# Hybrid retention and attention step on Trainium2: the last two feed-forward columns and the output phase in a written order

## The chip, the cores and the metric

The kernel is one program on one core of a Trainium2 chip. The metric is the device time of one execution in microseconds. The kernel before took 1125.89 us (median of 3 runs, 1125.66 to 1126.71). A core has TensorE for matmuls (PE in the profile, with PEld for its weight loads), VectorE (DVE), ScalarE (ACT) and GpSimd (POOL) for elementwise work, and SyncE (SP), which here only issues DMAs. Each engine works through a queue of its own in order, and waits on semaphores for the others.

## The reference, cut to what matters

640 tokens of width 1024 (128 of a prompt and 512 latent ones) go through one layer of a diffusion backbone. The change touches only its end: the gated feed-forward part with a convolution of width 3 over the tokens, its gated residual, and the last norm.

```python
def conv_ffn(h, w_up, conv_w, conv_b, w_down):
    L = h.shape[1]
    u = h @ w_up
    up = jnp.pad(u, ((0, 0), (1, 1), (0, 0)))
    uc = conv_w[0] * up[:, :L] + conv_w[1] * up[:, 1:L + 1] + conv_w[2] * up[:, 2:L + 2] + conv_b
    a, g = jnp.split(uc, 2, axis=-1)
    return (jax.nn.silu(g) * a) @ w_down
...
        xs = xs + g2 * conv_ffn(h, w_up[l], conv_w[l], conv_b[l], w_down[l])
...
    y_prompt = rmsnorm(xp, final_g)
    y_sample = rmsnorm(xs, final_g)
```

Here `rmsnorm(x, g)` is x times the reciprocal root of its mean square, times the weight g. The hidden width is 2816, so `w_up` has 2 x 2816 columns and `w_down` 2816 rows.

## The kernel before, in words

Matrices are multiplied in float32 as three products of split numbers (`mm3`, lines 158 to 161): each factor is a rounded high part and a low part that holds the rest. ScalarE makes the high part (a cast), and the low part is a difference, made by VectorE (L152), or by ScalarE and an adding DMA on GpSimd's queue (L149, L150; the argument `"dma"`).

The hidden width is cut into 22 columns of 128, numbered f = 0 to 21. For a column, the two halves of the up-projection (i = 0 the value, i = 1 the gate) are computed for pairs of columns by seven products of quarter matrices (`unit_group`, a Strassen-like scheme; products 1, 5, 6, 2, 3, 7, 4). Products 7 and 4 finish the two columns of a pair: product 7 the odd one, product 4 the even one. Then `conv(f, i)` does the convolution (one ScalarE step L1583, two VectorE steps L1584 and L1585), and `gate(f)` the gated product (tanh on ScalarE L1595, two VectorE steps L1596 and L1597, the high part on ScalarE L1598, the low part on VectorE L1599). The results feed the down-projection: five blocks of tokens t = 0 to 4 times two halves of the output width (c0 = 0 and 512). A bank of PSUM holds one such half (128 x 512).

`seq` is the written order of TensorE's work (`manual_schedule(engines={ET.PE})`). An engine that is named there keeps the order of the code; engines that are not named are ordered by the framework's planner, by readiness in its own estimate of times. While an item of `seq` runs, `pump` issues loads and splits of weights ahead, and `later` holds convolutions and gates that are popped one at a time. A unit's last product (product 4) is held back by two items of the next group.

The last four columns, 18 to 21, are multiplied at the end. `last_group(g)` accumulates the columns 18 and 19 (parts 0 and 1 of `fs`) for t = 0, 2, 1, 3 and both halves in eight banks while the gates of 20 and 21 are still being made. In the old order product 4 of the last unit comes after t=0 and t=2 of the first of these groups.

The output phase then has VectorE and TensorE in a written order. For each half, `last_mm` adds the columns 20 and 21 to the bank (`(4, ...)` has no bank yet and takes all four parts), `down_add` multiplies the bank by the residual gate `gb` into a temporary (L1671) and adds it to x1 (L1676), and `square` has ScalarE sum the squares (L1693, two rows of the profile). When all halves of a block are there, `root_sum` adds the partial sums (L1701), has GpSimd raise them to -0.5 (L1702) and VectorE scale them (L1703), and `root` refines that by one Newton step (L1710 to L1714). `out` stores a half: with `fused`, VectorE multiplies by the root and by the norm's weight `fg` in one step (L1725); otherwise ScalarE multiplies by the root alone (L1727), and the weight must have been multiplied in before, by `gain` on GpSimd (L1720). In the old order `gain` is done for three halves, (0, 0), (1, 0) and (2, 0), and seven halves are fused.

Of the kernel before, what the change touches and what calls it, by code (L numbers as in the profile page):

```python
# [9 lines left out]
F32 = mybir.dt.float32  # L10
# [8 lines left out]
P = 128  # L19
# [53 lines left out]
def hybrid_step(ctx: ExitStack, tc: tile.TileContext, a: dict, o: dict):  # L73
# [1506 lines left out]
    def conv(f, i):  # L1580
        u, q = ub[f % 2][i], i * NF + f
        v = cvs[f, i] = x_row()[:, :641]
        nc.scalar.activation(v, u[:, 1:642], AF.Identity, scale=cw[:, 1, q:q + 1], bias=cw[:, 3, q:q + 1])  # L1583
        V.scalar_tensor_tensor(v, u[:, 0:641], cw[:, 0, q:q + 1], v, op0=ALU.mult, op1=ALU.add)  # L1584
        V.scalar_tensor_tensor(v, u[:, 2:643], cw[:, 2, q:q + 1], v, op0=ALU.mult, op1=ALU.add)  # L1585

    gts = {}

    def gate(f):
        if f // 2 not in gts:  # L1590
            gts[f // 2] = gt_pair()
        r = [x[:, f % 2, 15:656] for x in gts[f // 2]]
        ca, cg = cvs[f, 0], cvs[f, 1]
        tg = t7([P, 641], tag="tg", bufs=1)
        nc.scalar.activation(tg, cg, AF.Tanh, scale=0.5)  # L1595
        V.scalar_tensor_tensor(cg, tg, 1.0, cg, op0=ALU.add, op1=ALU.mult)  # L1596
        V.tensor_mul(ca, ca, cg)  # L1597
        nc.scalar.copy(r[0], ca)  # L1598
        V.tensor_sub(r[1], ca, r[0].bitcast(F32))  # L1599

# [153 lines left out]
    def unit_group(p, i):  # L1754
# [34 lines left out]
        def prod(m):  # L1789
            def go():  # L1790
# [24 lines left out]
                elif m == 4:  # L1815
                    nc.scalar.copy(his[0], ps)
# [55 lines left out]
    def last_group(g):  # L1872
# [11 lines left out]

        def prep(h):
            def go():
                w = w_split(st["raw"][h], 2, 512, "dma" if h else None)
                ws[g] = [x + y for x, y in zip(ws.get(g, ([], [])), w)]
            return go

        items = [lambda t=t: last_mm(t, g * 512, 512, (0, 1)) for t in (0, 2, 1, 3)]
        return load, [(prep(0), 2, items)], items, prep(1)
# [3 lines left out]
    seq, held = [], []  # L1896
    for _, _, items in groups:
        for x in items[:-1] if len(items) == 7 else items:
# [4 lines left out]
        if len(items) == 7:  # L1903
            held.append((2, items[-1]))
# [21 lines left out]
    with tc.manual_schedule(engines={ET.PE}):  # L1926
        pump(0)
        for n, item in enumerate(seq):
# [7 lines left out]
    for fn in later:  # L1936
        fn()
    for e in ends:
        e[3]()

    fg = wp([P, 4 * 512], F32, tag="raw", bufs=2)[:, :DM]
    nc.sync.dma_start(fg, a["final_g"].unsqueeze(0).to_broadcast([P, DM]))
    with tc.manual_schedule(engines={ET.DVE, ET.PE}):
        def last(t, c0, n):
            last_mm(t, c0, n, (2, 3) if t < NT - 1 else (0, 1, 2, 3))
            down_add(bank[t, c0], t, c0)
            square(t, c0, n)
# [24 lines left out]
        out(3, 512, True)  # L1972
        out(3, 0, True)
# [37 lines left out]
```

## Time and profile before

| | us |
|---|---|
| median of 3 runs | 1125.89 |
| the profiled execution, its time | 1125.21 |
| the profiled execution, its span | 1123.3 |
| TensorE busy | 1098.1 |
| VectorE busy | 871.4 |
| ScalarE busy | 636.5 |
| GpSimd busy | 165.4 |

The span runs from the first to the last instruction of the profiled execution. In a row of the timeline, the first column is the start in microseconds from the span's start, the second the duration, then engine, line of the kernel, operation, output and inputs by the program's names, shape, and in brackets the idle time of the engine before it and what ended it. Engines overlap the end of one instruction with the start of the next, so starts can lie before the end of the row above.

### The profile page before, as it was taken

What the parts mean: (1) busy time and instruction counts of PE and PEld (TensorE: products, weight loads), DVE (VectorE), ACT (ScalarE), POOL (GpSimd) and SP (SyncE); (2) the same over time, 40 slices, a digit from 0 to 9 for tenths busy, and PEclk for the clock granted to TensorE, in tenths of its full rate; (3) what the DMA queues carried; (4) which work ended last, traced back from release to release, by engine and by line L of the source; (5) the groups of instructions that cost most, each with busy time, mean ns of one, the idle gap of its engine ahead of it and who ended that gap; (6) DMA issues with size and microseconds to landing.
All of it is one profiled execution on the core that took longest, in us unless ns stands there. A gap on an engine that the chain in (4) does not pass through costs nothing.

```text
span 1123.3 us, 17862 instructions
## 1 busy us (share of the span) xinstructions
PE 1098.1 (98%) x6757; PEld 1003.3 (89%) x6757; DVE 871.4 (78%) x1513; ACT 636.5 (57%) x1269; POOL 165.4 (15%) x190
## 2 busy tenths in 40 slices
PE   5999999999999999999999999999999999999996
PEld 4788899999989878899999889999899999899995
DVE  4677877668969969768887559968688597589888
ACT  5356656554234235768766336678466476575463
POOL 0042200000000011022113122012111111121012
PEclk9999999999999999999999999999999999999999
DMA  9742111016855726746669837457657656676552
GB/s 306 254 142 84 42 39 38 1 38 215 287 190 155 245 72 141 98 75 123 129 134 187 293 133 178 114 117 145 147 131 175 132 97 148 132 132 167 124 131 94
DMA packets 147109, 156.85 MB, mean 140 GB/s; under 512 B 28216, under 2 KB 117384, under 8 KB 146768
## 3 DMA queue, kind: packets, MB, share of 16 engines
q1 hardware_dynamic: 110880, 119.65, 33.8%
q0 software_dynamic: 35872, 35.95, 20.7%
q8 instruction: 53, 0.87, 0.3%
q14 instruction: 32, 0.26, 0.1%
q10 hardware_dynamic: 272, 0.11, 0.0%
HBM read 115.71 MB, written 8.67 MB: 111 GB/s over the span
## 4 chain that ended last, share of the span: by engine, by line
PE 90%; DVE 4%; ACT 2%; DMA 2%; issue 1%; SPq 1%; ACTq 0%; DVEq 0%
DMA p0.u4.4_116<-in_w_mod 1%; DVE x1.u1.1_6541 L1676 1%; DMA weights.raw.266_7937<-in_w_down 0%; DMA xin.u1.1_72<-in_c_ctx 0%; SPq L331 0%; DVE x1.u1.1_6541 L1725 0%; PE mm3.mm.57_5730 L1149 0%; DVE x1.u1.1_6541 L1483 0%; PE mm3.mm.72_6381 L1149 0%; DVE acts.u2.2_91 L432 0%; PE mm1.mm.11_294 L161 0%; PE mm7.mm.8_7748 L1799 0%; PE mm3.mm.69_6246 L1152 0%; PE mm3.mm.66_6117 L1152 0%; PE mm7.mm.50_10241 L1798 0%
## 5 line engine op out<-in xcount | busy, mean ns | idle before, releaser
L816 POOL DMA_DIRECT2D spill.u2.2_2891<-f1.s.1_1160 x1 | 0.6, 592 | 129.8 <-DVE mod.u3.3_2846 L604 129.8
L1813 DVE TENSOR_TENSOR t7.u4.4_7029<-t7.u4.4_7029,const.u1.1_70 128x320 f32<-128x320 f32 x10 | 4.9, 493 | 11.0 <-ACT const.u1.1_70 L1812 11.0
L429 ACT CAST acts.u1.1_90<-f0.s.2_104 128x640 fp32r<-128x640 f32 x4 | 2.9, 728 | 9.5 <-DVE f0.s.2_104 L427 9.5
L152 DVE TENSOR_TENSOR weights.wh.113_4462<-weights.raw.111_4459,weights.wh.112_4461 128x1024 fp32r<-128x1024 f32 x1 | 1.2, 1226 | 8.6 <-ACT weights.wh.112_4461 L147 8.6
L299 POOL DMA_DIRECT2D mod.acc.25_3630<-in_b_mod x2 | 1.7, 848 | 42.2 <-ACT ret.u4.4_3422 L874 42.2
L584 POOL TENSOR_TENSOR p1.u1.1_604<-p1.u3.3_608,p1q.u1.1_598 128x512 f32<-128x512 f32 x1 | 1.3, 1311 | 44.1 <-DMA p1.vc.6_613<-in_cache_v 44.1
L1001 DVE SCALAR_TENSOR_TENSOR ret2.u1.1_4272<-ret2.u1.1_4272,const.u10.10_86 64x128 f32<-64x128 f32 x24 | 6.6, 381 | 1.2 <-ACT ret2.u1.1_4272 L994 1.1
L147 ACT CAST weights.wh.67_3284<-weights.raw.66_3282 128x1024 fp32r<-128x1024 f32 x1 | 1.0, 1048 | 11.3 <-PE mm3.mm.8_3125 L198 11.3
L147 ACT CAST weights.wh.77_3520<-weights.raw.76_3518 128x1024 fp32r<-128x1024 f32 x1 | 1.1, 1051 | 11.2 <-PE mm3.mm.16_3382 L198 11.2
L553 ACT ACTIVATE f0.s.3_710<-f0.s.3_710,p1q.ny20.11_878 128x128 f32<-128x128 f32 x20 | 6.0, 389 | 2.5 <-DVE p1q.ny20.11_878 L220 2.5
L553 ACT ACTIVATE p1.u4.4_610<-p1.u4.4_610,p1.ny10.15_660 128x128 f32<-128x128 f32 x10 | 3.0, 388 | 7.6 <-DVE p1.ny10.15_660 L220 7.6
L429 ACT CAST acts.u1.1_90<-f0.s.1_103 128x640 fp32r<-128x640 f32 x4 | 2.9, 726 | 7.8 <-DVE f0.s.1_103 L427 7.7
L446 PE MATMUL aux1.aux.1_134<-const.u1.1_70,xin.u1.1_72 80*128 80x80 f32 x1 | 0.4, 367 | 7.0 <-DMA xin.u1.1_72<-in_b_mod 7.0
L999 DVE SCALAR_TENSOR_TENSOR ret2.u1.1_4272<-ret2.u1.1_4272,const.u10.10_86 64x128 f32<-64x128 f32 x24 | 6.7, 336 | 0.5 <-ACT ret2.u1.1_4272 L992 0.5
L1235 ACT ACTIVATE rt.u1.1_5123<-rt.u1.1_5123 128x640 f32<-128x640 f32 x8 | 5.9, 740 | 1.5 <-DVE rt.u1.1_5123 L1163 1.5
L1720 POOL TENSOR_TENSOR x1.u1.1_6541<-x1.u1.1_6541,weights.raw.441_11100 128x512 f32<-128x512 f32 x3 | 4.9, 1636 | 12.2 <-ACT x1.tm.111_11113 L1693 9.4
L1687 DVE TENSOR_TENSOR x1.u1.1_6541<-x1.u1.1_6541,gate.u1.1_6527 128x512 f32<-128x512 f32 x10 | 6.7, 685 | 0.0
L269 ACT ACTIVATE mod.wm.41_4253<-aux3.aux.5_4243 128x512 f32<-128x512 f32 x1 | 0.6, 597 | 10.6 <-issue 10.6
L446 PEld LDWEIGHTS aux1.aux.1_134<-const.u1.1_70,xin.u1.1_72 80*128 80x128 f32 x1 | 0.2, 182 | 7.0 <-issue 7.0
L152 DVE TENSOR_TENSOR weights.wh.83_3656<-weights.raw.81_3653,weights.wh.82_3655 128x1024 fp32r<-128x1024 f32 x1 | 1.2, 1226 | 6.6 <-ACT weights.wh.82_3655 L147 6.6
L299 POOL DMA_DIRECT2D mod.acc.34_3970<-in_b_mod x2 | 1.5, 759 | 31.7 <-PE mm3.mm.31_3941 L161 31.5
L553 ACT ACTIVATE f0.s.4_959<-f0.s.4_959,p1q.ny20.20_1127 128x128 f32<-128x128 f32 x20 | 6.2, 399 | 0.0
(6860 smaller groups left out, 5029.7 us busy)
## 6 DMA issues: line engine op xcount, KB each, us to landing
spill.u1.1_2890<-x1.u1.1_6541 POOLq DMA_DIRECT2D x5, 512.0 KB, 3.8
xin.u2.2_102<-in_x_sample SPq DMA_DIRECT2D x4, 512.0 KB, 4.6
p0.u5.5_119<-in_w_mod SPq DMA_DIRECT2D x2, 1024.0 KB, 9.7
p0.u6.6_125<-in_w_mod SPq DMA_DIRECT2D x2, 1024.0 KB, 14.2
p0.u7.7_128<-in_w_mod SPq DMA_DIRECT2D x2, 1024.0 KB, 12.3
gate.u1.1_6527<-spill.u3.3_2892 SPq DMA_DIRECT2D x2, 1024.0 KB, 10.9
x1.u1.1_6541<-in_x_sample SPq DMA_DIRECT2D x4, 512.0 KB, 6.9
out_y_sample<-x1.u1.1_6541 SPq DMA_DIRECT2D x8, 256.0 KB, 2.2
```

The lines of the kernel that those rows point to most:

```text
L147: nc.scalar.copy(hi, rv)
L152: (lo_eng or V).tensor_sub(lo, rv, hi.bitcast(F32))
L299: nc.gpsimd.dma_start(accs[v][0:1, c, :], a["b_mod"][0:1, col:col + DM], accum_op=ALU.add)
L429: nc.scalar.copy(hT[0][:, k, :], xk)
L553: nc.scalar.activation(x[:, j], x[:, j], AF.Copy, scale=rstd[:, j:j + 1])
L999: V.scalar_tensor_tensor(Ss[0:64, hh, st + 1, j], Ss[0:64, hh, st, j], cdsel[0:64, h:h + 1], Ss[0:64, hh, st + 1, j], op0=ALU.mult, op1=AL ...
L1001: V.scalar_tensor_tensor(Ss[64:128, hh, 2 - st, j], Ss[64:128, hh, 3 - st, j], cdsel[64:128, h:h + 1], Ss[64:128, hh, 2 - st, j], op0=ALU. ...
L1235: nc.scalar.activation(x, x, AF.Tanh, scale=0.5)
L1676: V.tensor_add(x1[:, t, gs], x1[:, t, gs], down_mul(ps, t, c0))
L1687: V.tensor_mul(x1[:, t, gs], x1[:, t, gs], gb[:, t == 0, gs])
L1720: eng.tensor_mul(x, x, fg[:, c0:c0 + 512])
L1813: V.tensor_sub(his[1], his[1], u3[i])
```

## The change

It has three parts. First, `conv` and `gate` are cut into generators, so that their steps can be interleaved; for the last two columns the tanh goes into the tile `ub` of the column's own up-projection, in place of the one tile `tg`. Second, the last two columns are written out in a fixed order for TensorE, VectorE and ScalarE: product 7, the item t=0 of the first group, product 4, then the steps of the two columns in turn; the second half of the last weights is split by ScalarE and VectorE in that order (`prep_parts`) instead of by ScalarE and the adding DMA. The half (3, 512) isn't begun ahead any more, so its columns 18 and 19 are multiplied in the output phase. Third, the output phase has another order, now for ScalarE too, and `gain` is done for six halves: (0, 0), (1, 0), (2, 0), (2, 512), (3, 0) and (4, 0); four halves are fused.

```diff
-    def conv(f, i):
+    def conv_parts(f, i):
         u, q = ub[f % 2][i], i * NF + f
         v = cvs[f, i] = x_row()[:, :641]
         nc.scalar.activation(v, u[:, 1:642], AF.Identity, scale=cw[:, 1, q:q + 1], bias=cw[:, 3, q:q + 1])
+        yield
...
+    def conv(f, i):
+        run(conv_parts(f, i))
...
-    def gate(f):
+    def gate_parts(f):
...
-        tg = t7([P, 641], tag="tg", bufs=1)
+        tg = t7([P, 641], tag="tg", bufs=1) if f + 2 < NF else ub[f % 2][1][:, 1:642]
         nc.scalar.activation(tg, cg, AF.Tanh, scale=0.5)
+        yield
         V.scalar_tensor_tensor(cg, tg, 1.0, cg, op0=ALU.add, op1=ALU.mult)
         V.tensor_mul(ca, ca, cg)
+        yield
         nc.scalar.copy(r[0], ca)
+        yield
         V.tensor_sub(r[1], ca, r[0].bitcast(F32))
...
-                    if i and (p % 2 == 0 or p == 1):
+                    if i and (p % 2 == 0 or p == 1) and f0_ + 2 < NF:
                         later.extend([lambda: gate(f0_ + 1), lambda: gate(f0_)])
...
+        def prep_parts():
+            rv = st["raw"][1][:, :1024]
+            hi, lo = (wp([P, 1024], F32R, tag="wh", bufs=8) for _ in range(2))
+            nc.scalar.copy(hi, rv)
+            yield
+            V.tensor_sub(lo, rv, hi.bitcast(F32))
+            put([[x[:, :512], x[:, 512:]] for x in (hi, lo)])
+
+        items = [lambda t=t: last_mm(t, g * 512, 512, (0, 1)) for t in ((0, 2, 1, 3), (0, 2, 1))[g]]
+        return load, [(prep(0), 2, items)], items, prep_parts() if g else prep(1)
...
-        for n, item in enumerate(seq):
+        cut = pos[id(last_unit[-2])]
+        for n, item in enumerate(seq[:cut]):
...
+        for fn in later:
+            fn()
+        later.clear()
+        pump(cut + 2)
+        assert not preps and loaded == len(groups)
+        ends[0][3]()
...
+    with tc.manual_schedule(engines={ET.PE, ET.DVE, ET.Activation}):
+        seq[cut]()
+        f1_, f0_ = NF - 1, NF - 2
+        c1_ = conv_parts(f1_, 1)
+        next(c1_)
+        seq[cut + 2]()
+        seq[cut + 1]()
+        c0_ = conv_parts(f0_, 1)
+        next(c0_)
+        next(ends[1][3])
+        run(c1_)
+        g1_ = gate_parts(f1_)
+        next(g1_)
+        run(c0_)
+        g0_ = gate_parts(f0_)
+        next(g1_)
+        next(g0_)
+        next(g1_)
+        next(g0_)
+        run(g1_)
+        next(g0_)
+        run(g0_)
+        run(ends[1][3])
+        for item in seq[cut + 3:]:
+            item()
...
         for t in range(3):
-            last(t, 0, 512)
+            down_part(t, 0, 512)
             gain(t, 0, nc.gpsimd)
-            last(t, 512, 512)
-        last(3, 0, 512)
+        for t in range(3):
+            down_part(t, 512, 512)
+        gain(2, 512, nc.gpsimd)
+        down_part(3, 0, 512)
+        gain(3, 0, nc.gpsimd)
         root_sum(0, 3)
-        last(3, 512, 512)
         root(0, 3)
         out(0, 0)
-        last(4, 0, 512)
         out(1, 0)
+        down_part(3, 512, 512)
+        out(2, 0)
+        out(2, 512)
+        out(0, 512, True)
+        out(1, 512, True)
         root_sum(3, 1)
-        out(0, 512, True)
-        last(4, 512, 256)
-        last(4, 768, 256)
-        out(2, 0)
+        down_part(4, 0, 512)
+        gain(4, 0, nc.gpsimd)
         root(3, 1)
-        out(1, 512, True)
+        out(3, 0)
+        down_part(4, 512, 256)
+        out(3, 512, True)
+        down_part(4, 768, 256)
         root_sum(4, 1)
-        out(2, 512, True)
         root(4, 1)
+        out(4, 0)
         out(4, 512, True)
-        out(4, 0, True)
-        out(3, 512, True)
-        out(3, 0, True)
```

`down_part` is the old `last` (the matmuls of a half, `down_add`, `square`); it takes all four parts where the half has no bank yet.

More of the change, by code (lines that the diff above doesn't have):

```diff
@@ L1896, in hybrid_step @@
     seq, held = [], []
+    last_unit = groups[-3][2]
     for _, _, items in groups:
-        for x in items[:-1] if len(items) == 7 else items:
+        for x in items[:-1] if len(items) == 7 and items is not last_unit else items:
             seq.append(x)
@@ L1902, in hybrid_step @@
                 seq.append(held.pop(0)[1])
-        if len(items) == 7:
+        if len(items) == 7 and items is not last_unit:
             held.append((2, items[-1]))
@@ L1935, in hybrid_step @@
                 later.pop(0)()
[L1936 to L1947, printed above, removed]
+        for fn in later:
+            fn()
```

17 lines of the change are left out of this document (11 added, 6 removed).

## The prediction

> **What bounds the kernel now.** I read the page first (engine totals, then the chain that ended last), then the windows of the output phase, then the timelines of the engines around it. The page says that TensorE is the bound of nearly the whole span:
>
> ```profile
> PE 1098.1 (98%) x6757; PEld 1003.3 (89%) x6757; DVE 871.4 (78%) x1513; ACT 636.5 (57%) x1269; POOL 165.4 (15%) x190
> PE 90%; DVE 4%; ACT 2%; DMA 2%; issue 1%; SPq 1%; ACTq 0%; DVEq 0%
> ```
>
> The change touches only the last 40 us, so what counts is which engine ends last there. The windows view (busy time and, in brackets, instructions) splits the output phase; of its rows, the part up to the first `root` and the tail after the last `down_add`:
>
> ```profile
> 1098.75:1110.87 12.12, 12.12 (x54) 9.78 (x53) 11.77 (x19) 5.07 (x14) 5.80 (x4) 1.00 0.01 1
> ...
> 1115.28:1123.30 8.02, 0.00 (x0) 0.00 (x0) 4.86 (x12) 0.51 (x2) 0.55 (x1) 0.66 0.61 231
> ```
>
> VectorE is busy for 11.77 of the first 12.12 us, while GpSimd has 5.80 and ScalarE 5.07: this phase belongs to VectorE, and the tail to VectorE, then to the last stores. Its start is set by TensorE, whose timeline has no gap before it:
>
> ```profile
> 1088.66 0.31 PE L1799 MATMUL mm7.mm.59_10879<-acts.u1.1_90,weights.wh.434_10917 128*128 128x320 f32 x1
> ...
> 1095.78 0.39 PE L159 MATMUL mm7.mm.65_11082<-weights.wh.435_10951,gt.gt0.25_10753 128*128 128x512 f32 x1
> ...
> 1097.17 0.39 PE L159 MATMUL acc7.acc.51_11002<-weights.wh.437_11090,gt.gt0.27_11040 128*128 128x512 f32 x1
> ...
> 1098.55 0.39 PE L159 MATMUL acc7.acc.53_11061<-weights.wh.439_11095,gt.gt0.27_11040 128*128 128x512 f32 x1
> ```
>
> Six matmuls make half a bank, 1.39 us (1095.78 to 1097.17 to 1098.55). VectorE's timeline then shows how the handover goes and what one half costs it:
>
> ```profile
> 1097.10 0.83 DVE L1599 TENSOR_TENSOR gt.gt1.28_11041<-x1.row.107_10933,gt.gt0.27_11040 128x641 fp32r<-128x641 f32 x1 [0.79 <-ACT gt.gt0.27_11040 L1598]
> 1098.75 0.69 DVE L1671 TENSOR_TENSOR x1.tm.110_11110<-acc7.acc.51_11002,gate.u1.1_6527 128x512 f32<-128x512 f32 x1 [0.82 <-PE acc7.acc.51_11002 L161]
> 1099.48 0.69 DVE L1676 TENSOR_TENSOR x1.u1.1_6541<-x1.u1.1_6541,x1.tm.110_11110 128x512 f32<-128x512 f32 x1
> 1100.14 0.69 DVE L1671 TENSOR_TENSOR x1.tm.112_11122<-acc7.acc.53_11061,gate.u1.1_6527 128x512 f32<-128x512 f32 x1
> ```
>
> The last gate result is there at 1097.93, so VectorE waits for TensorE (0.82 us), and from 1098.75 it needs 1.39 us a half (1098.75 to 1100.14) for the L1671 multiply and the L1676 add. Third, GpSimd's products by `fg` are not free for VectorE:
>
> ```profile
> 641.69 1.29 POOL L1483 TENSOR_TENSOR x1.u1.1_6541<-x1.u1.1_6541,x1.tm.4_6631 128x512 f32<-128x512 f32 x1 [8.47 <-DVE x1.tm.4_6631 L1482]
> ...
> 1101.06 1.65 POOL L1720 TENSOR_TENSOR x1.u1.1_6541<-x1.u1.1_6541,weights.raw.441_11100 128x512 f32<-128x512 f32 x1 [9.39 <-ACT x1.tm.111_11113 L1693]
> 1107.19 1.60 POOL L1720 TENSOR_TENSOR x1.u1.1_6541<-x1.u1.1_6541,weights.raw.441_11100 128x512 f32<-128x512 f32 x1 [1.44 <-ACT x1.tm.119_11159 L1693]
> ```
>
> ```profile
> 1108.27 1.08 DVE L1676 TENSOR_TENSOR x1.u1.1_6541<-x1.u1.1_6541,x1.tm.122_11179 128x512 f32<-128x512 f32 x1
> 1109.27 0.15 DVE L1701 TENSOR_REDUCE t7.rm.28_11184<-x1.u3.3_6543 128x3 f32<-128x12 f32 x1
> ...
> 1110.87 0.16 DVE L1712 TENSOR_TENSOR t7.rt.31_11201<-t7.ry.30_11186 128x3 f32<-128x3 f32 x1
> ```
>
> A 512-wide product takes GpSimd 1.29 us where VectorE leaves it alone, 1.65 and 1.60 here: it first waits for the running L1676. The next L1676 (1108.27) takes 1.08 instead of 0.69 and ends 0.56 after GpSimd's end (1107.19 + 1.60 = 1108.79). The two engines exclude each other when both read two tiles of SBUF; L1671, which reads PSUM, runs on beside GpSimd. So seven halves with three products take 1109.35 - 1098.75 = 10.60 us.
>
> **The change, part by part. 1: TensorE.** The item t=3 of the second group goes, and its six matmuls come back in front of `(3, 512)`. The output phase starts one half earlier: 1098.75 - 1.39 = **1097.36**. The moved matmuls cost nothing: TensorE would end `(3, 512)` at 1097.16 + 8 halves of 1.39 = 1108.3, and VectorE, as worked out below, wants it at 1111.8.
>
> **2: the two columns.** The start holds only if the gates keep up. Rows of the old order:
>
> ```profile
> 1084.77 1.05 ACT L147 CAST weights.wh.439_11095<-weights.raw.433_10900 128x1024 fp32r<-128x1024 f32 x1
> 1085.72 0.93 ACT L1583 ACTIVATE x1.row.108_10998<-t7.u4.4_7029,const.u13.13_89 128x641 f32<-128x641 f32 x1
> 1089.17 0.41 ACT L1816 COPY t7.u2.2_7027<-mm7.mm.59_10879 128x320 f32<-128x320 f32 x1
> ...
> 1090.44 0.91 ACT L1583 ACTIVATE x1.row.109_11029<-t7.u2.2_7027,const.u13.13_89 128x641 f32<-128x641 f32 x1
> 1093.84 0.74 ACT L1595 ACTIVATE t7.tg.27_11055<-x1.row.109_11029 128x641 f32<-128x641 f32 x1 [1.87 <-DVE x1.row.109_11029 L1585]
> ```
>
> ```profile
> 1079.90 1.22 DVE L152 TENSOR_TENSOR weights.wh.436_10952<-t7.rawl.25_10898,weights.wh.435_10951 128x1024 fp32r<-128x1024 f32 x1
> ...
> 1087.60 0.89 DVE L1585 SCALAR_TENSOR_TENSOR x1.row.108_10998<-t7.u4.4_7029,const.u13.13_89,x1.row.108_10998 128x641 f32<-128x641 f32 x1
> ```
>
> Before, a cast stood ahead of either convolution: that of 1084.77 before 1085.72, and a second between 1089.17 and 1090.44. Now product 4 ends one half sooner, 1088.97 - 1.39 = 1087.6; its copy 0.41, the convolution 0.93 and one cast 1.05 bring ScalarE to 1090.0, the first tanh to 1090.7. VectorE does the two L1585-like steps of column 20 by 1090.8 (0.89 each), the gate of column 21 by 1092.5 (0.83 a step, as L1599), that of column 20 by 1094.1, the two low parts by 1094.9 and 1095.7. TensorE wants column 21 at 1095.8 and column 20's low part, in its third matmul, at 1097.0. Product 4 also takes the bank of product 7 again; that one's copy (0.41) is hidden by the 1.39 of the item t=0 between them. The weights' low part, now on VectorE instead of GpSimd's DMA, costs 1.22 (L152) and ends at 1096.9, before the first output multiply. All hidden, with 0.5 to 1.2 us to spare; beyond that, each microsecond late is a microsecond of start. The tanh tile put into `u` waits for nothing new: the convolution has read it by then. The `fg` load waits for the same buffer as before and stays hidden by the six halves.
>
> **3: up to the first root.** Seven halves with three products again: the last L1676 ends at 1097.36 + 10.60 = 1107.96, the sixth one about 1.39 sooner, 1106.57. A product starts 0.89 after its add's end (1099.48 + 0.69 to 1101.06, the square between), so the product of `(2, 512)` runs from 1107.46 for 1.65 to 1109.11. Behind it on GpSimd's queue stand the product of `(3, 0)` and the power of `root_sum(0, 3)`:
>
> ```profile
> 1109.50 0.89 POOL L1702 TENSOR_TENSOR t7.ry.30_11186<-t7.rm.28_11184,const.u1.1_70 128x3 f32<-128x3 f32 x1 [0.71 <-DVE t7.rm.28_11184 L1701]
> ```
>
> That power took 0.89 on an idle GpSimd. The planner, not the diff, orders the two. If the product is first, the power ends at 1109.11 + 1.29 + 0.89 = 1111.3. If the power is first, it ends at 1110.0 and the product follows at once, while `root`'s first instruction (L1712) reads two tiles. Who then gets the port is shown by an older place, where a GpSimd instruction releases VectorE and has another behind it:
>
> ```profile
> 97.53 1.90 POOL L562 TENSOR_TENSOR p1q.sw.14_911<-f0.s.3_710,p1q.u3.3_600 128x256 f32<-128x256 f32 x2
> ```
>
> ```profile
> 97.61 1.22 DVE L564 TENSOR_TENSOR f0.s.3_710<-f0.s.3_710,p1q.u2.2_599 128x512 f32<-128x512 f32 x1 [2.05 <-POOL p1q.sw.13_902 L562]
> 98.86 1.12 DVE L565 TENSOR_TENSOR f0.s.3_710<-f0.s.3_710,p1q.sw.13_902 128x512 f32<-128x512 f32 x1
> ```
>
> The VectorE step starts at 97.61, after GpSimd's next one, and takes 1.22 where one of 512 takes 0.68 to 0.69: it is held. So root starts at 1111.3 either way. Before, L1671 and L1676 of `(3, 512)` stood between `root_sum` and `root` and covered the power; now nothing does, and the written order holds VectorE from 1108.2 to 1111.3, **3.1 us**, with every `down_part`, and behind it ScalarE's first `out`, queued up. With 0.49 for root (1110.87 to 1111.36 below) `(3, 512)` starts at 1111.8.
>
> **4: the rest.**
>
> ```profile
> 1111.36 0.69 DVE L1671 TENSOR_TENSOR x1.tm.126_11220<-acc7.acc.55_11207,gate.u1.1_6527 128x512 f32<-128x512 f32 x1
> ...
> 1113.61 0.42 DVE L1671 TENSOR_TENSOR x1.tm.128_11248<-acc7.acc.56_11235,gate.u1.1_6527 128x256 f32<-128x256 f32 x1
> ...
> 1114.40 0.42 DVE L1671 TENSOR_TENSOR x1.tm.130_11266<-acc7.acc.57_11253,gate.u1.1_6527 128x256 f32<-128x256 f32 x1
> 1114.85 0.43 DVE L1676 TENSOR_TENSOR x1.u1.1_6541<-x1.u1.1_6541,x1.tm.130_11266 128x256 f32<-128x256 f32 x1
> 1115.20 0.21 DVE L1710 SCALAR_TENSOR_TENSOR t7.rt.35_11273<-t7.ry.34_11229,t7.rh.33_11228 128x1 f32<-128x1 f32 x1
> 1115.52 0.75 DVE L1725 SCALAR_TENSOR_TENSOR x1.u1.1_6541<-x1.u1.1_6541,t7.ry.30_11186,weights.raw.441_11100 128x512 f32<-128x512 f32 x1
> 1116.18 0.15 DVE L1701 TENSOR_REDUCE t7.rm.36_11278<-x1.u3.3_6543 128x1 f32<-128x4 f32 x1
> 1116.44 0.74 DVE L1725 SCALAR_TENSOR_TENSOR x1.u1.1_6541<-x1.u1.1_6541,t7.ry.30_11186,weights.raw.441_11100 128x512 f32<-128x512 f32 x1
> ...
> 1117.54 1.41 DVE L1725 SCALAR_TENSOR_TENSOR x1.u1.1_6541<-x1.u1.1_6541,t7.ry.38_11280,weights.raw.441_11100 128x512 f32<-128x512 f32 x2
> 1118.88 1.41 DVE L1725 SCALAR_TENSOR_TENSOR x1.u1.1_6541<-x1.u1.1_6541,t7.ry.34_11229,weights.raw.441_11100 128x512 f32<-128x512 f32 x2
> ```
>
> `(3, 512)` 1.39; two fused outputs at 0.66 (1115.52 to 1116.18); `root_sum` 0.26 (1116.18 to 1116.44); `(4, 0)` 1.39; root 0.32 (1115.20 to 1115.52); `(4, 512)` 0.79 (1113.61 to 1114.40): 1111.8 + 5.47 = 1117.3, its add still running to 1117.35. GpSimd's product of `(4, 0)` has waited since about 1117.1. In the row at 98.86 the waiting GpSimd instruction came between two VectorE steps (1.12 instead of 0.68), so I take it to come first: to 1118.65, then the rest of the fused output 0.56 and `(4, 768)` 0.88 (two steps of 0.43 and a gap) less an overlap of 0.07. The last add ends at 1120.0; were VectorE never held, at 1118.8. From there the tail has one fused output left. ScalarE's last row of the old tail is the end of the square:
>
> ```profile
> 1115.70 0.19 ACT L1693 ACTIVATION_READ_ACCUMULATOR x1.tm.131_11269<-x1.u1.1_6541 128x1 f32 x1
> ```
>
> So: 0.61 from the last add's end to the square's (1115.28 to 1115.89), 0.08 to the reduce, 1.36 from reduce to fused output (1116.18 to 1117.54), 0.75 for it, and 3.01 from VectorE's last end to the span's end (1118.88 + 1.41 = 1120.29 to 1123.30): 5.81. Here the change gains: the old tail took 8.02 (1115.28 to 1123.30), since three more fused outputs stood in it.
>
> **Sum:** 1120.0 + 5.8 = 1125.8, against 1123.3: -1.4 by the start, -2.2 by the tail, +3.1 by the wait, the rest by fused outputs moved ahead and by held steps. That is 2.5 us more. The profiled execution took 1125.21 (1.91 outside its span), the median is 1125.89: **1128.3 us, slower by 0.2%**.
>
> The Trainium skill, GPSIMD Engine Reference, section 3.1, gives about 2.6 cycles an element for a two-input step of GpSimd, at 1.2 GHz an estimate of 1.11 us for 512; three products stand in my chain, so the sum would be 0.5 us lower by it. The trace has 1.29, and I stay with that.
>
> **The rivals.** (a) VectorE keeps the port and GpSimd's last product fits beside L1671: end of adds 1118.8, **1127.1 us**. For it: VectorE's steps start 0.07 before the old one ends. Against: the row at 98.86. (b) Not slower: the power comes first on GpSimd and L1712 gets the port before the product behind it. Root starts at 1110.1, 1.2 sooner, less 0.4 for an add held as at 1108.27: **1127.5**, with (a) **1126.3**, no change. It decides at one point, whether VectorE's first instruction after the power starts before GpSimd's next; the row at 97.61 speaks against it. The Trainium skill, SBUF — State Buffer, section "Who interferes with whom", says that the first to start holds the shared port for its whole instruction; the held rows agree, and leave open who is first. (c) Faster: GpSimd holds nobody up, because the power is placed ahead of the product of `(2, 512)` and nothing is held: seven halves take 7 x 1.39 = 9.7, root starts at 1108.2, the adds end 7.5 later at 1115.7, and the last two stores, which no longer follow two others within 2.75 us, may land 0.5 sooner (an estimate): **1123.6**. Against it: the product is ready 0.6 us before the power. (d) The columns are late by more than they have to spare, because the written order makes one engine wait for another at each step: +1.5 us, **1129.8**.
>
> **Chances.** Forecast 0.43 (from 1127.6 to 1129.0; by 0.30 above the line), (a) 0.17, (b) 0.13, (c) 0.14 (0.11 of it faster), (d) 0.13. A measurement of this kernel tells about 0.2%, 2.25 us, from no change. Slower: 0.30 + 0.13 = 0.43; faster 0.11; the same 0.46, since the forecast stands close to the line. The range from 1124.9 to 1129.9 leaves out most of (c) and half of (d).
>
> **What would show it.** Right: the first L1671 near 1097.4; a gap of VectorE near 3 us between `root_sum(0, 3)` and L1712, released by GpSimd; a fused output of over 1 us beside GpSimd's sixth product; 5.8 us from the last add to the end. Wrong: L1712 within 1 us of the reduce, products of GpSimd with no longer VectorE step beside them, or a gap of TensorE before the output phase.

## The result, and the profile after

| | us |
|---|---|
| before, median of 12 runs | 1125.89 (1125.46 to 1126.97) |
| changed, median of 12 runs | 1128.66 (1127.81 to 1128.88) |
| ratio | 1.0022, 95% interval 1.0013 to 1.0031 |
| changed, the profiled execution, its time and its span | 1128.41 and 1126.5 |

The changed kernel is 2.77 us (0.2%) slower. Line numbers have moved: the multiply by the gate is L1681 (L1671 before), its add L1686, the square L1703, the steps of `root_sum` L1711 (reduce), L1712 (power, GpSimd) and L1713 (scale), those of `root` L1720 and L1722 to L1724, the product by `fg` on GpSimd L1730, the fused output L1735, ScalarE's output L1737, the store L1739.

From the page of the changed kernel, the engine totals and the chain that ended last:

```profile
PE 1099.1 (98%) x6757; PEld 1004.1 (89%) x6757; DVE 873.1 (78%) x1511; ACT 639.0 (57%) x1271; POOL 170.0 (15%) x192
PE 89%; DVE 4%; ACT 3%; issue 1%; DMA 1%; POOL 0%; ACTq 0%; SPq 0%; POOLq 0%; DVEq 0%
```

GpSimd has 4.6 us more than before (three more products), VectorE 1.7 more, although three fused outputs went: the low part of the last weights has come to it (1.22, the row of 1096.31 below), and a held instruction counts as busy. The windows of the output phase, cut at the first step of `root` and at the end of the last add, as before:

```profile
1098.07:1110.70 12.63, 12.63 (x56) 10.19 (x55) 11.46 (x16) 5.08 (x14) 7.55 (x6) 1.00 0.01 1
1110.70:1120.17 9.47, 4.06 (x30) 3.63 (x28) 9.19 (x18) 5.01 (x11) 3.12 (x3) 0.95 0.51 194
1120.17:1126.50 6.33, 0.00 (x0) 0.00 (x0) 1.44 (x5) 1.23 (x3) 0.55 (x1) 0.50 0.33 124
```

The first window hardly grew (12.63 against 12.12 us), but it holds seven halves and a wait where it held eight halves; the tail fell from 8.02 to 6.33, and the middle doubled, from 4.41 to 9.47. From the first multiply to the span's end it is 28.43 us where it was 24.55, 3.88 more, of which the earlier start gives back 1.4.

VectorE's timeline shows where the time is (L1906 is the low part of the last weights, the last step of the two columns):

```profile
1096.31 1.22 DVE L1906 TENSOR_TENSOR weights.wh.440_11031<-weights.raw.432_10881,weights.wh.439_11030 128x1024 fp32r<-128x1024 f32 x1
...
1098.07 0.69 DVE L1681 TENSOR_TENSOR x1.tm.110_11100<-acc7.acc.51_11008,gate.u1.1_6527 128x512 f32<-128x512 f32 x1 [0.54 <-PE acc7.acc.51_11008 L161]
...
1107.98 0.69 DVE L1686 TENSOR_TENSOR x1.u1.1_6541<-x1.u1.1_6541,x1.tm.122_11170 128x512 f32<-128x512 f32 x1
1108.59 0.16 DVE L1711 TENSOR_REDUCE t7.rm.26_11176<-x1.u3.3_6543 128x3 f32<-128x12 f32 x1
1108.78 1.08 DVE L1713 TENSOR_SCALAR t7.rh.27_11177<-t7.rm.26_11176 128x3 f32<-128x3 f32 x1
1110.70 1.25 DVE L1722 TENSOR_TENSOR t7.rt.29_11182<-t7.ry.28_11178 128x3 f32<-128x3 f32 x1 [0.84 <-POOL t7.ry.28_11178 L1712]
1111.98 0.16 DVE L1723 TENSOR_TENSOR t7.rt.29_11182<-t7.rt.29_11182,t7.rh.27_11177 128x3 f32<-128x3 f32 x1
...
1112.26 0.68 DVE L1681 TENSOR_TENSOR x1.tm.124_11203<-mm7.mm.65_11190,gate.u1.1_6527 128x512 f32<-128x512 f32 x1
...
1113.59 1.41 DVE L1735 SCALAR_TENSOR_TENSOR x1.u1.1_6541<-x1.u1.1_6541,t7.ry.28_11178,weights.raw.441_11092 128x512 f32<-128x512 f32 x2
...
1117.61 1.76 DVE L1735 SCALAR_TENSOR_TENSOR x1.u1.1_6541<-x1.u1.1_6541,t7.ry.32_11218,weights.raw.441_11092 128x512 f32<-128x512 f32 x1
...
1119.74 0.43 DVE L1686 TENSOR_TENSOR x1.u1.1_6541<-x1.u1.1_6541,x1.tm.130_11279 128x256 f32<-128x256 f32 x1
...
1122.07 0.75 DVE L1735 SCALAR_TENSOR_TENSOR x1.u1.1_6541<-x1.u1.1_6541,t7.ry.36_11286,weights.raw.441_11092 128x512 f32<-128x512 f32 x1
```

and GpSimd's, beside it, shows who holds it up:

```profile
1108.24 1.59 POOL L1730 TENSOR_TENSOR x1.u1.1_6541<-x1.u1.1_6541,weights.raw.441_11092 128x512 f32<-128x512 f32 x1 [2.77 <-ACT x1.tm.121_11161 L1703]
1109.78 0.89 POOL L1712 TENSOR_TENSOR t7.ry.28_11178<-t7.rm.26_11176,const.u1.1_70 128x3 f32<-128x3 f32 x1
1110.64 1.28 POOL L1730 TENSOR_TENSOR x1.u1.1_6541<-x1.u1.1_6541,weights.raw.441_11092 128x512 f32<-128x512 f32 x1
...
1117.47 1.35 POOL L1730 TENSOR_TENSOR x1.u1.1_6541<-x1.u1.1_6541,weights.raw.441_11092 128x512 f32<-128x512 f32 x1 [1.78 <-ACT x1.tm.127_11238 L1703]
```

The sum of squares is there at 1108.75 (1108.59 + 0.16), but the power starts only when the product of `(2, 512)` has ended, at 1109.78. The next product starts 0.03 us before the power's recorded end (1110.67), and L1722, two tiles of three numbers, runs from 1110.70 to 1111.95; the product ends at 1111.92. The same instruction took 0.16 before. So 3.2 us pass between the reduce and the end of L1722 (1108.75 to 1111.95), in which VectorE, in its written order, has only the short L1713 to do besides. That one is held as well (1.08 at 1108.78; 0.17 at the same place in four of the kernels below), within that time. Near the end the fused output at 1117.61 takes 1.76 beside the product of `(4, 0)`; the next multiply starts 1.68 later instead of 0.66.

These pieces carry the difference. The last add ends 22.10 us after the first multiply, before 16.53: 5.57 more. From the end of the seventh add to the next multiply it is 3.59 us (1108.67 to 1112.26), where the steps of `root_sum` and `root` took 0.68 when the power was covered (0.19 and 0.49): the wait is 2.9 of the 5.57. Three fused outputs stand ahead of the last add instead of one (2 x 0.66 + 1.68 against 0.66: 2.3), and the second `root` (0.3), which stood behind it. The tail gives 1.69 back and the start 1.4.

One part of the two spans' difference isn't the change's. TensorE's first matmul of the item t=0, ahead of everything that the change touches:

```profile
1084.25 0.39 PE L159 MATMUL acc7.acc.51_11002<-weights.wh.431_10894,gt.gt0.25_10753 128*128 128x512 f32 x1
```

```profile
1084.98 0.39 PE L159 MATMUL acc7.acc.51_11008<-weights.wh.433_10916,gt.gt0.25_10753 128*128 128x512 f32 x1
```

The changed kernel's profiled execution was already 0.73 us later here. Between the kernels below the first multiply varies as much with the same code ahead of it (1097.83 in one, 1098.54 in another). So times are compared from the first multiply on, and the span's +3.2 is 2.5 of the change and 0.7 of the two executions.

### The profile page after: what moved, and what is told of

The parts are those of the page before. It is cut to its first block, busy times and chain, and to the rows that moved or that the text cites. A ratio compares the mean times of both kernels' runs of the same rounds, so it can differ in the third digit from the quotient of the medians.

```text
span 1126.5 us, 17864 instructions
## 1 busy us (share of the span) xinstructions
PE 1099.1 (98%) x6757; PEld 1004.1 (89%) x6757; DVE 873.1 (78%) x1511; ACT 639.0 (57%) x1271; POOL 170.0 (15%) x192
## 4 chain that ended last, share of the span: by engine, by line
PE 89%; DVE 4%; ACT 3%; issue 1%; DMA 1%; POOL 0%; ACTq 0%; SPq 0%; POOLq 0%; DVEq 0%
DMA ret2.qd.16_4823<-ret.u4.4_3422 0%; DMA weights.raw.266_7937<-in_w_down 0%; DVE x1.u1.1_6541 L1686 0%; DMA xin.u1.1_72<-in_b_mod 0%; POOL x1.u1.1_6541 L1730 0%; PE mm3.mm.57_5730 L1149 0%; DVE x1.u1.1_6541 L1483 0%; PE mm3.mm.72_6381 L1149 0%; DVE acts.u2.2_91 L432 0%; PE mm1.mm.11_294 L161 0%; PE mm3.mm.57_5730 L1152 0%; PE mm3.mm.69_6246 L1152 0%; PE mm3.mm.66_6117 L1152 0%; PE mm7.mm.44_9987 L1808 0%; PE mm7.mm.41_9754 L1809 0%
## 5 line engine op out<-in xcount | busy, mean ns | idle before, releaser
L1730 POOL TENSOR_TENSOR x1.u1.1_6541<-x1.u1.1_6541,weights.raw.441_11092 128x512 f32<-128x512 f32 x6 | 9.3, 1569 | 19.3 <-ACT x1.tm.111_11103 L1703 14.7
```

Of the source, the lines that this page charges most:

```text
L1730: eng.tensor_mul(x, x, fg[:, c0:c0 + 512])
```

## The experiments

The theory (A) is the prediction's: the power stands behind a product on GpSimd's queue, `root`'s first step then loses the port to the product behind the power, the sixth product holds a fused output, and the columns cost nothing. One rival (Q) has GpSimd's queue alone to blame: VectorE waits for the power and is not held by a port. The other (C) has the columns' fixed order cost time that the output phase hides or shows. All diffs are against the changed kernel, except the second, which is against the kernel before. The kernel before took 1126.14 us (median of 27 runs) beside the first four experiments and 1126.13 (33 runs) beside the last four; their ratios are to these.

**The columns alone.** The columns as changed, the output phase in the old order, VectorE and TensorE alone written out in it:

```diff
+    with tc.manual_schedule(engines={ET.DVE, ET.PE}):
         for t in range(3):
             down_part(t, 0, 512)
             gain(t, 0, nc.gpsimd)
-        for t in range(3):
             down_part(t, 512, 512)
-        gain(2, 512, nc.gpsimd)
         down_part(3, 0, 512)
-        gain(3, 0, nc.gpsimd)
         root_sum(0, 3)
+        down_part(3, 512, 512)
         root(0, 3)
...
```

> The two columns in the written order and (3, 512) not begun ahead, but the output phase in the old order (three products, VectorE and TensorE written, ScalarE planned). Theory A (the loss sits in the new output order, the columns are hidden): the first L1681 multiply comes 1.4 us earlier, but TensorE has as much to do as before and ends (4, 0) at the same time as before, so VectorE, which now stands 1.4 us earlier in its order, waits for it there; ratio to before 0.9985 to 1.0005, about 1125.5 us. From the first multiply to the end of the span 25.5 to 26.0 us (24.55 before). Rival C (the written order of the columns costs): ratio 1.001 or more, with a gap of TensorE before the output phase.

Measured: 1126.02 us, ratio 0.9999 (0.9990 to 1.0008): the time of before. The first multiply comes at 1098.17, earlier, and nothing of it is left at the end. VectorE's and TensorE's timelines say why:

```profile
1109.31 0.69 DVE L1681 TENSOR_TENSOR x1.tm.124_11196<-mm7.mm.65_11183,gate.u1.1_6527 128x512 f32<-128x512 f32 x1 [0.27 <-PE mm7.mm.65_11183 L161]
...
1112.16 0.69 DVE L1681 TENSOR_TENSOR x1.tm.126_11220<-acc7.acc.55_11207,gate.u1.1_6527 128x512 f32<-128x512 f32 x1 [0.97 <-ACT x1.u1.1_6541 L1737]
```

```profile
1111.66 0.40 PE L161 MATMUL acc7.acc.55_11207<-weights.wh.437_10984,gt.gt1.28_11036 128*128 128x512 f32 x1
1111.89 0.28 PE L159 MATMUL acc7.acc.56_11235<-weights.wh.435_10951,gt.gt0.25_10753 128*128 128x256 f32 x1
```

VectorE now waits for TensorE, 0.27 us at `(3, 512)` and 0.97 at `(4, 0)`. The profile names ScalarE as what ended the second wait, but the L1737 that it names works on the halves of t = 0 to 2, and before, the same multiply started at 1111.36, ahead of the first of those steps (L1727, 1111.67), so it doesn't need them. The last matmul of its own bank starts only at 1111.66 and ends, by its row, at 1112.06. The matmuls taken from ahead of the phase come back in it: the multiply of `(4, 0)` comes 13.99 us after the first one, before it was 12.61 (1111.36 - 1098.75), so the 1.38 us of the start are used up there. The columns cost nothing that this interval shows, and their 1.4 us alone don't gain anything either.

**The output phase alone.** The old columns, the new order of the output phase; `(3, 512)` stays begun ahead:

```diff
-    with tc.manual_schedule(engines={ET.DVE, ET.PE}):
-        def last(t, c0, n):
-            last_mm(t, c0, n, (2, 3) if t < NT - 1 else (0, 1, 2, 3))
+    with tc.manual_schedule(engines={ET.PE, ET.DVE, ET.Activation}):
+        def down_part(t, c0, n):
+            last_mm(t, c0, n, (2, 3) if (t, c0) in bank else (0, 1, 2, 3))
...
-            last(t, 512, 512)
-        last(3, 0, 512)
+        for t in range(3):
+            down_part(t, 512, 512)
+        gain(2, 512, nc.gpsimd)
+        down_part(3, 0, 512)
+        gain(3, 0, nc.gpsimd)
         root_sum(0, 3)
-        last(3, 512, 512)
         root(0, 3)
...
```

> The old columns with the new output phase (six products, ScalarE written too; (3, 512) begun ahead as before). Theory A: the same holds at the first root and beside the last product as in the changed kernel, 28.0 to 28.4 us from the first multiply to the end, and the first multiply 1.4 us later than in the changed kernel: 1129.5 to 1130.2 us, ratio to before 1.003 to 1.004. Rival C: 1126 us or less, since the loss belongs to the columns.

Measured: 1129.98 us (5 runs, the others have 11), ratio 1.0033 (1.0020 to 1.0045), the slowest of all. Its VectorE has the line numbers of before:

```profile
1111.81 1.25 DVE L1712 TENSOR_TENSOR t7.rt.31_11192<-t7.ry.30_11188 128x3 f32<-128x3 f32 x1 [0.85 <-POOL t7.ry.30_11188 L1702]
...
1118.72 1.76 DVE L1725 SCALAR_TENSOR_TENSOR x1.u1.1_6541<-x1.u1.1_6541,t7.ry.34_11221,weights.raw.441_11100 128x512 f32<-128x512 f32 x1
```

L1712 is held for 1.25 and the fused output for 1.76, as in the changed kernel, and from the first multiply to the end it is 28.43 us in both. So the whole loss is in the output phase. With the old columns it is 3.84 us (1129.98 - 1126.14), with the new ones 2.77: here VectorE, not TensorE, sets the pace, and the columns' earlier start is worth about a microsecond by the medians (1.4 by the rows).

**Cover for the power.** `(3, 512)` back between `root_sum` and `root`, with all six products:

```diff
         root_sum(0, 3)
+        down_part(3, 512, 512)
         root(0, 3)
         out(0, 0)
         out(1, 0)
-        down_part(3, 512, 512)
         out(2, 0)
```

> The changed kernel with down_part(3, 512) moved between root_sum(0, 3) and root(0, 3). Theory A (the power waits behind a product, and then root's first instruction is held by the next product): (3, 512) fills 1.4 us of the wait, root's first step L1722 is still held by the product of (3, 0) and ends at the same place, 13.9 us after the first multiply; 1127.2 us, 1.3 to 1.5 below the changed kernel. Rival Q (only the queue of GpSimd delays root; the port plays no part): L1722 takes 0.2 us and the time falls by 2.4 us or more, to 1126.2.

Measured: 1127.54 us, ratio 1.0013 (1.0004 to 1.0022). VectorE and GpSimd:

```profile
1108.55 1.09 DVE L1713 TENSOR_SCALAR t7.rh.27_11177<-t7.rm.26_11176 128x3 f32<-128x3 f32 x1
1109.55 0.68 DVE L1681 TENSOR_TENSOR x1.tm.124_11195<-mm7.mm.65_11182,gate.u1.1_6527 128x512 f32<-128x512 f32 x1
1110.26 0.69 DVE L1686 TENSOR_TENSOR x1.u1.1_6541<-x1.u1.1_6541,x1.tm.124_11195 128x512 f32<-128x512 f32 x1
1110.87 1.27 DVE L1722 TENSOR_TENSOR t7.rt.29_11200<-t7.ry.28_11178 128x3 f32<-128x3 f32 x1
```

```profile
1109.56 0.88 POOL L1712 TENSOR_TENSOR t7.ry.28_11178<-t7.rm.26_11176,const.u1.1_70 128x3 f32<-128x3 f32 x1
1110.41 1.71 POOL L1730 TENSOR_TENSOR x1.u1.1_6541<-x1.u1.1_6541,weights.raw.441_11092 128x512 f32<-128x512 f32 x1
```

The power ends at 1110.44 while VectorE is busy, so the queue holds nobody up, and L1722 starts without any idle time before it. It still takes 1.27 us, beside the product of `(3, 0)`. That product in its turn took 1.71 instead of 1.28: it first had to let the add of 1110.26 end. The queue alone (Q) has no reason for a held L1722 here. The cover takes the wait away, and the holds stay: that of L1722, and that of L1713 (1.09), which now keeps the multiply of `(3, 512)` waiting. The expectation had left that one out: L1722 ends 14.31 us after the first multiply, not 13.9, and the time falls by 1.1 us, not by 1.3 to 1.5.

**No product of `(3, 0)`.** That half is fused instead:

```diff
-        gain(3, 0, nc.gpsimd)
         root_sum(0, 3)
...
-        out(3, 0)
+        out(3, 0, True)
```

> The changed kernel with the product of (3, 0) taken off GpSimd: that half is stored by a fused step of VectorE instead. Theory A: nothing is behind the power on GpSimd, so L1722 takes 0.2 instead of 1.25 us and (3, 512) starts 1.1 us sooner after the first multiply; the fused step costs 0.66 back, so the time falls by 0.4 us, to 1128.2. Rival Q: L1722 keeps its 1.25 us, and the time rises by 0.7.

Measured: 1127.91 us, ratio 1.0016 (1.0007 to 1.0025).

```profile
1110.88 0.16 DVE L1722 TENSOR_TENSOR t7.rt.29_11181<-t7.ry.28_11177 128x3 f32<-128x3 f32 x1 [0.85 <-POOL t7.ry.28_11177 L1712]
...
1117.14 1.04 DVE L1686 TENSOR_TENSOR x1.u1.1_6541<-x1.u1.1_6541,x1.tm.128_11258 128x256 f32<-128x256 f32 x1
```

With no product behind the power, L1722 takes 0.16: the hold goes with that product. The multiply of `(3, 512)` comes 13.14 us after the first one, 1.05 sooner than in the changed kernel. Some 0.65 of it remain to the end: there is a fused output more, and the sixth product, no longer beside a fused output, holds the add of `(4, 512)` instead (1.04 where 0.43 is usual). That hold is 0.6 us where the fused output's was 1.0, which the expectation hadn't counted; the time came out 0.3 below it.

**The power first.** GpSimd in written order too, with the power ahead of both products:

```diff
+    with tc.manual_schedule(engines={ET.PE, ET.DVE, ET.Activation, ET.Pool}):
         for t in range(3):
...
-        gain(2, 512, nc.gpsimd)
         down_part(3, 0, 512)
-        gain(3, 0, nc.gpsimd)
         root_sum(0, 3)
+        gain(2, 512, nc.gpsimd)
+        gain(3, 0, nc.gpsimd)
         root(0, 3)
```

> The changed kernel with GpSimd in the written order too for the output phase, and there the power of root_sum(0, 3) ahead of the products of (2, 512) and (3, 0). The power no longer waits in GpSimd's queue, but both products now stand right behind it. Theory A (after the power the next product takes the port first, and a step of VectorE that reads two tiles waits for its whole length): L1722 is held by the first product and L1723 by the second, 1.2 us each; (3, 512) starts 14.2 to 14.6 us after the first multiply (14.2 in the changed kernel), and the time is that of the changed kernel within 0.4 us. Rival Q (the queue alone): L1722 and L1723 take 0.2 us each, (3, 512) starts at 12.2, and the time falls by 1.6 us or more.

Measured: 1128.43 us, ratio 1.0019 (1.0011 to 1.0028): no gain over the changed kernel.

```profile
1109.13 0.88 POOL L1712 TENSOR_TENSOR t7.ry.28_11179<-t7.rm.26_11177,const.u1.1_70 128x3 f32<-128x3 f32 x1 [3.36 <-DVE t7.rm.26_11177 L1711]
1109.99 2.54 POOL L1730 TENSOR_TENSOR x1.u1.1_6541<-x1.u1.1_6541,weights.raw.441_11092 128x512 f32<-128x512 f32 x2
```

```profile
1109.09 0.17 DVE L1713 TENSOR_SCALAR t7.rh.27_11178<-t7.rm.26_11177 128x3 f32<-128x3 f32 x1
1110.05 1.25 DVE L1722 TENSOR_TENSOR t7.rt.29_11185<-t7.ry.28_11179 128x3 f32<-128x3 f32 x1 [0.79 <-POOL t7.ry.28_11179 L1712]
1111.33 1.22 DVE L1723 TENSOR_TENSOR t7.rt.29_11185<-t7.rt.29_11185,t7.rh.27_11178 128x3 f32<-128x3 f32 x1
```

The power is done at 1110.01, 11.66 us after the first multiply, 0.94 earlier than in the changed kernel. The two products follow it, and each holds one step of `root`: L1722 takes 1.25 and L1723 takes 1.22. L1713, which here has no product beside it, takes 0.17 again. The multiply of `(3, 512)` comes 14.31 us after the first one, where Q asks for 12.2. This speaks against Q once more, and it answers what the prediction left to the planner: the order on GpSimd did not matter, because in both orders the product queued behind the power got in ahead of VectorE's step that the power releases.

**No product of `(2, 512)` and `(3, 0)`.** Both are fused:

```diff
-        gain(2, 512, nc.gpsimd)
         down_part(3, 0, 512)
-        gain(3, 0, nc.gpsimd)
...
-        out(2, 512)
+        out(2, 512, True)
...
-        out(3, 0)
+        out(3, 0, True)
```

> The changed kernel with the products of (2, 512) and (3, 0) both taken off GpSimd; the two halves are stored by fused steps of VectorE. Theory A: the power follows the reduce at once, L1722 comes 11.7 us after the first multiply instead of 12.6 and takes 0.2 us, L1713 takes 0.17 instead of 1.08, (3, 512) starts at 12.2 instead of 14.2; two fused steps cost 1.3 back: 1127.3 to 1128.1 us. Rival Q gives the same start and so the same time; it has to differ from the run without the product of (3, 0) alone by the power's wait, 0.9 us earlier.

Measured: 1127.57 us, ratio 1.0011 (1.0003 to 1.0020).

```profile
1109.68 0.16 DVE L1722 TENSOR_TENSOR t7.rt.29_11180<-t7.ry.28_11176 128x3 f32<-128x3 f32 x1 [0.79 <-POOL t7.ry.28_11176 L1712]
...
1111.47 2.07 DVE L1735 SCALAR_TENSOR_TENSOR x1.u1.1_6541<-x1.u1.1_6541,t7.ry.28_11176,weights.raw.441_11092 128x512 f32<-128x512 f32 x3
```

Nothing is queued ahead of the power or behind it, and the multiply of `(3, 512)` comes at 12.15 us after the first one, 2.04 sooner than in the changed kernel (14.19) and 0.99 sooner than in the run without the product of `(3, 0)` alone. Both theories ask for that, so this run doesn't tell them apart. A wait of 0.79 for the power itself stays, since nothing covers it. Half of the 2.04 is lost again: three fused outputs in a row instead of two, that of `(3, 0)` later, and the add of `(4, 512)` held (1.03).

**No product of `(4, 0)`.** That half is fused, and its output goes last:

```diff
-        gain(4, 0, nc.gpsimd)
         root(3, 1)
...
         root(4, 1)
-        out(4, 0)
         out(4, 512, True)
+        out(4, 0, True)
```

> The changed kernel with the last product, that of (4, 0), taken off GpSimd; the half is stored by a fused step of VectorE at the very end. Theory A (the product holds the fused step of (3, 512)): that step takes 0.75 instead of 1.76 us, the last add ends 1.0 us sooner after the first multiply, 21.1 instead of 22.1; the added fused step costs 0.66 at the end: 1128.0 to 1128.4 us. Rival: the fused step is long for another reason and keeps its length; then 1129.3.

Measured: 1127.47 us, ratio 1.0012 (1.0003 to 1.0021), 0.5 or more better than expected.

```profile
1118.11 0.74 DVE L1735 SCALAR_TENSOR_TENSOR x1.u1.1_6541<-x1.u1.1_6541,t7.ry.32_11218,weights.raw.441_11092 128x512 f32<-128x512 f32 x1
...
1121.56 1.41 DVE L1735 SCALAR_TENSOR_TENSOR x1.u1.1_6541<-x1.u1.1_6541,t7.ry.36_11285,weights.raw.441_11092 128x512 f32<-128x512 f32 x2
```

The fused output at 1118.11 takes 0.74 instead of 1.76, as it should. The rest is at the end, which the expectation had left as it was: the two last halves (the row of 1121.56) get ready one after the other, 0.67 us apart, and the store of the first is issued while the second is still being computed. The span ends 2.93 us after VectorE's last end; in the changed kernel it is 3.68 (1122.82 to 1126.50), because there both last halves are ready at 1122.8 and SyncE issues their stores one behind the other. ScalarE's last row and SyncE's queue in the changed kernel, SyncE's here, and SyncE's in the kernel before:

```profile
1122.13 0.72 ACT L1737 ACTIVATE x1.u1.1_6541<-x1.u1.1_6541,t7.ry.36_11286 128x512 f32<-128x512 f32 x1 [1.36 <-DVE t7.ry.36_11286 L1724]
```

```profile
1122.87 0.81 SPq L1739 DMA_DIRECT2D out_y_sample<-x1.u1.1_6541  x2
```

```profile
1122.33 1.00 SPq L1739 DMA_DIRECT2D out_y_sample<-x1.u1.1_6541  x2
```

```profile
1118.32 2.32 SPq L1729 DMA_DIRECT2D out_y_sample<-x1.u1.1_6541  x4
```

In the changed kernel the last issue ends 0.86 us after VectorE's last end (1123.68 against 1122.82); here it is 0.36 (1123.33 against 1122.97), and before it was 0.35 (1120.64 against 1120.29). That is 0.5 of the 0.75; the rest lies between the last issue and the span's end (2.57 against 2.82), and no run shows why.

**A mixed version.** From what these show: products only early, where GpSimd is idle and nothing waits for it (five, all of t = 0 and 1 and the first half of t = 2); `(3, 512)` as cover for the first power; fused outputs in the waits of the last root; `(4, 0)` without a product:

```diff
-        for t in range(3):
+        for t in range(2):
             down_part(t, 0, 512)
             gain(t, 0, nc.gpsimd)
-        for t in range(3):
             down_part(t, 512, 512)
-        gain(2, 512, nc.gpsimd)
+            gain(t, 512, nc.gpsimd)
+        down_part(2, 0, 512)
+        gain(2, 0, nc.gpsimd)
+        down_part(2, 512, 512)
         down_part(3, 0, 512)
-        gain(3, 0, nc.gpsimd)
         root_sum(0, 3)
+        down_part(3, 512, 512)
         root(0, 3)
...
+        out(2, 512, True)
         root_sum(4, 1)
+        out(3, 512, True)
         root(4, 1)
-        out(4, 0)
         out(4, 512, True)
+        out(4, 0, True)
+        out(3, 0, True)
```

> The columns of the changed kernel with another output order: products on GpSimd for (0, 0), (0, 512), (1, 0), (1, 512) and (2, 0), all behind halves whose VectorE step of the next half reads PSUM; (3, 512) between root_sum(0, 3) and root(0, 3); the fused steps of (2, 512) and (3, 512) in the two waits of the last root. Theory A: VectorE loses 0.4 us a product but only where TensorE would make it wait anyway, the root is not held, and one fused step less than before stands in the tail: 0.6 to 1.2 us below the kernel before, 1124.7 to 1125.3. If the five products in a row hold VectorE beyond TensorE's pace: 1126 or more.

Measured: 1124.86 us, ratio 0.9988 (0.9979 to 0.9997), 1.3 us below the kernel before and the only one whose interval lies below 1. GpSimd, VectorE and the window of the tail:

```profile
1100.35 8.49 POOL L1730 TENSOR_TENSOR x1.u1.1_6541<-x1.u1.1_6541,weights.raw.441_11092 128x512 f32<-128x512 f32 x5 [14.74 <-ACT x1.tm.111_11103 L1703]
1109.54 0.88 POOL L1712 TENSOR_TENSOR t7.ry.28_11178<-t7.rm.26_11176,const.u1.1_70 128x3 f32<-128x3 f32 x1 [0.70 <-DVE t7.rm.26_11176 L1711]
```

```profile
1098.03 0.69 DVE L1681 TENSOR_TENSOR x1.tm.110_11100<-acc7.acc.51_11008,gate.u1.1_6527 128x512 f32<-128x512 f32 x1 [0.54 <-PE acc7.acc.51_11008 L161]
...
1110.90 0.15 DVE L1722 TENSOR_TENSOR t7.rt.29_11200<-t7.ry.28_11178 128x3 f32<-128x3 f32 x1
...
1114.83 0.42 DVE L1681 TENSOR_TENSOR x1.tm.130_11272<-acc7.acc.57_11259,gate.u1.1_6527 128x256 f32<-128x256 f32 x1 [0.21 <-PE acc7.acc.57_11259 L161]
1115.29 0.42 DVE L1686 TENSOR_TENSOR x1.u1.1_6541<-x1.u1.1_6541,x1.tm.130_11272 128x256 f32<-128x256 f32 x1
```

```profile
1115.71:1122.80 7.09, 0.00 (x0) 0.00 (x0) 4.00 (x10) 0.63 (x4) 0.55 (x1) 0.67 0.68 259
```

The five products are over at 1108.84, before the reduce of `root_sum` (1109.31), so the power starts at once and L1722 takes 0.15. They hold five adds (0.94 to 1.08 where 0.69 is usual), so seven halves take 11.36 us instead of 10.60. As expected, nothing of that reaches the end, because VectorE waits for TensorE again before the last bank (0.21 at 1114.83). The last add ends 17.68 us after the first multiply, before 16.53: most of the start's 1.4 us goes there, since TensorE is what the last bank waits for. What remains is 0.25, and 0.93 in the tail, 7.09 us where it was 8.02, with one fused output less behind the last add and the second `root` ahead of it.

## Why the prediction was right, point by point

The forecast was 1128.3, the measured median is 1128.66, and the mechanism is the one forecast. Since the profiled execution was 0.73 late before the change's first instruction, times of after are given here less 0.73.

- **TensorE and the start.** Predicted 1097.36, found 1097.34 (1098.07 - 0.73), with VectorE waiting for TensorE, 0.54 us. The columns alone came out at the time of before, and no gap of TensorE appears ahead of the output phase: the columns are hidden, as forecast. Rival (d) is out.
- **Up to the first root.** Seven halves took 10.60 us as forecast. The power stands between the two products, an order that was left open with the claim that it doesn't matter; the run with the power first confirms the claim. From the reduce's end to the next multiply it is 3.51 us (1108.75 to 1112.26), predicted 3.6 (1108.2 to 1111.8). The gap of 3 us that was named as a sign came in two pieces: 1.95 us to the start of L1722, and the 1.25 for which it was held. Rivals (b) and (c), which need `root`'s first step (L1712 before, L1722 now) to get in ahead of the product, or nothing to be held, are refuted by the rows of that step (1.25 to 1.27) in five kernels with a product behind the power, and 0.15 to 0.16 in the four without.
- **The rest.** The sixth product came between two steps of VectorE and stretched the fused output to 1.76, predicted about 1.9; without that product 0.74. Rival (a) is out.
- **Two terms were mis-sized, and cancel.** The last add ended at 1119.44 (1120.17 - 0.73), not 1120.0: the forecast let `root` start at 1111.3 and then ran its first step once more, although a held step is over when its holder ends (0.27 us, with the 0.1 by which that product ended sooner), and the steps from `(3, 512)` to `(4, 768)` were priced 0.29 too high: 0.12 in two halves at 1.39 that took 1.33, the rest at the held fused output. The tail from the last add to the end is 6.33, not 5.81, so the sign of 5.8 us did not come: the steps up to the fused output took 0.15 less, but the span ends 3.68 after VectorE's last end, where 3.01 was carried over from before. That 3.01 belongs to a tail in which the stores get ready one by one; the new order makes ScalarE and VectorE finish the last two halves at the same moment (1122.85 and 1122.82), and SyncE issues one store after the other, 0.5 us. The other 0.16 is the time from the last issue's end to the span's end (2.82 against 2.66). So the sum was 0.56 too long in one place and 0.52 too short in another; that it came out within 0.1 us (1126.5 less 0.73, against 1125.8) is luck.

The Trainium skill, SBUF — State Buffer, section "Who interferes with whom", says that whoever issues first has the shared port pair for its whole instruction, and lists `tensor_scalar` among the operations that can enter a two-port mode and so contend with GpSimd. The trace agrees in both for the 512-wide products: L1722 ends 0.03 us after its holder, and L1713, one input of three numbers, takes 1.08 us beside a product and 0.17 without one. What it leaves open, who is first when a GpSimd instruction releases VectorE and has another behind it, came out for GpSimd in all five kernels that have a product there.

What wasn't tried is a GpSimd instruction in that place which reads no SBUF; so the runs show that the product holds VectorE's steps, and not by themselves that it is the port.

## What to carry to other kernels

An engine that shares something with another isn't idle capacity: put its bulk work where nobody waits for it, keep it away from a short step that a third engine's chain needs, and count what stands before and behind that step in its queue, since a product behind it held a three-number step for its full length in both orders tried. When a wait is covered by independent work, moving that work is a cost even if nothing is added. An earlier start gains only if the engine that provides it isn't needed again later for the work that was moved.

## What the hardware showed that was not expected

- A VectorE step with one SBUF input (L1713, 128x3) was held by a product on GpSimd for 1.08 us, where 0.17 is usual; the prediction had counted only steps with two inputs as exposed. In the changed kernel that cost nothing, because the power was later still; with the power covered it lay on the path.
- Two stores that get ready together cost 0.5 us at the very end: SyncE issues them one behind the other, two in 0.81 us, and the span's end follows the second.
- The profile named ScalarE as what ended a wait of VectorE for TensorE (the 0.97 us at 1112.16 in the run with the columns alone); the last matmul of that bank, whose row ends at 1112.06, showed that it was TensorE.
- Not every GpSimd instruction holds VectorE for the length of its row: a power of one number a row (0.55 us, the row below, in the kernel before) starts 0.03 us ahead of the fused output of 1116.44, which keeps its usual 0.74. The run with the columns alone and the mixed one show the same.

```profile
1116.41 0.55 POOL L1702 TENSOR_TENSOR t7.ry.38_11280<-t7.rm.36_11278,const.u1.1_70 128x1 f32<-128x1 f32 x1 [2.94 <-DVE t7.rm.36_11278 L1701]
```
